# Attention's last ten units as five two-head units with side-by-side products, and the chain's preparation moved behind the first half of a step

## The chip, the cores and the metric

One core of a Trainium2 chip. The metric is device time of one execution in microseconds (us), the median of several runs. A core has TensorE (PE, matrix products out of SBUF into PSUM), VectorE (DVE), ScalarE (ACT), GpSimd (POOL) and SyncE (SP, which issues most DMA transfers). Each engine works through its own instructions in order and waits for semaphores of the others.

## The reference, cut to what matters

A two-layer backbone on 2048 latent and 256 context tokens. Each layer projects its input, runs a state-space scan (SSD), a gated delta rule (GDN) and attention beside each other, and multiplies the mix with `w_out`. Attention has 6 query heads of 64 over 2 key heads; GDN runs over chunks of 64 in both directions.

```python
def _attend(q, k, v):          # per block of 128 queries
    s = jnp.einsum('bqhgd,bkhd->bhgqk', qi, k) * scale
    pr = jax.nn.softmax(s, axis=-1)
    return jnp.einsum('bhgqk,bkhd->bqhgd', pr, v)

def step(S, inp):              # GDN, one chunk of 64
    v_new = u_i - jnp.einsum('bhcd,bhde->bhce', w_i, S)
    o = jnp.einsum('bhcd,bhde->bhce', qd, S) + jnp.einsum('bhij,bhje->bhie', a_i, v_new)
    S = S * d_i[..., None, None] + jnp.einsum('bhcd,bhce->bhde', kd, v_new)
```

## The kernel before, in words

Everything is fp32. A product on TensorE is either fp32, which the trace shows as two records per product, or fp32r, one record. Where more precision than one fp32r product gives is wanted, an operand is split into a rounded part and a remainder, and three fp32r products take the place of one fp32 product.

**Order of the work.** The program is emitted by Python loops. A planner then simulates it with its own costs and fixes each engine's order ahead of the run: of the instructions that are ready in its simulation it takes the one emitted first, those under `tc.high_priority()` ahead. `behind(a, b)` (L1002) adds an order between two instructions of one engine without a semaphore. Pools give each tile name a number of buffers (`bufs`); a tile waits for the release of the buffer before it.

**Attention** (L645) has 24 units per layer, one for each head and block of 512 queries, over 18 key tiles of 128. (Layer 0 has six small ones for the context tokens too.) For each unit `unit_max` (L515) loads the queries (`q2`, three buffers), lets GpSimd copy 64 rows of them to `qm` (L522), computes rough scores (`pq`, L531), takes their maxima on VectorE (`mx`, L533; `nm`, L535, L536), and turns the negative maxima into a row by four fp32 products with a one-column operand (`pm`, L541), which VectorE copies into row 64 of `qm` (L542). `unit_main` (L545) then goes over the key tiles: two score products (L562, L563), the exponential on ScalarE (`pe`, L565), and the product with the values (`po`, L556). The values have a 65th column of ones, which gives the row sums. For units 0 to 12 the value product is one fp32 product of a 65-column operand; for units 13 to 23 ScalarE rounds `pe` to `ph` (L570), VectorE makes the remainder `pl` (L571), and three fp32r products follow. The next unit's `unit_max` is advanced between a unit's key tiles. The scores and rough scores share three PSUM banks in the chain's stage.

**Around it.** Units 0 to 7 are emitted behind gating, `gdn_pre`, `gdn_solve`, `ssd_states` (its state product L789 writes two 64-column halves) and `ssd_out`; then comes `gdn_chain` (L1006), and the rest of the units behind it. So attention fills what these leave.

**The chain** goes over 18 tiles, both directions at once. In round u it emits the loads of tile u+2 (`load`, L1038, three buffers for `kqc`, `er`, `acv`), then `prep` of tile u+1 (L1058), then `step` of tile u (L1088). `prep` multiplies keys and queries by decays (L1060 on VectorE, L1062 and L1064 on GpSimd), masks `acv` (L1065 on VectorE), and completes an inverse by 32 small products (L1071, L1080) with ScalarE copies (L1075, L1083). `step` has two halves: products with the state (L1104), a subtraction (L1108), products (L1113, L1118), a copy (L1123), products (L1127, L1129), and the state's update on VectorE (L1131); GpSimd scales the old state (L1106).

The output product (L1238) of all tiles follows when the chain and attention allow.

Of the kernel before, what the change touches and what calls it, by code (L numbers as in the profile page):

```python
# [17 lines left out]
P = 128  # L18
# [16 lines left out]
GT = 768  # L35

# [48 lines left out]
def hybrid_kernel(ctx, tc, x, c, ctx_in, c_ctx, norm_w, w_mod, b_mod, w_in, conv_w, conv_b, ssd_A_log,  # L85
# [158 lines left out]
    for l in range(DEPTH):  # L244
# [246 lines left out]
        with ExitStack() as bx:  # L491
            splx = bx.enter_context(ExitStack())
            ap_ = splx.enter_context(tc.tile_pool(reuse_waits="tile", name="ap", bufs=2))
            spl = splx.enter_context(tc.tile_pool(reuse_waits="tile", name="spl", bufs=2))
            vh = []
# [19 lines left out]

            def unit_max(h, q0, qn, k0t, k1t, st):
# [4 lines left out]
                qm = ap_.tile([65, 512], F32R, name="qm", bufs=3)  # L521
                nc.gpsimd.tensor_copy(qm[0:64, :qn], q2[0:64, :qn].bitcast(F32))  # L522
# [3 lines left out]
                nm = ap_.tile([P, 4], F32, name="nm")  # L526
                for u in range(qn // P):
                    mx = ap_.tile([P, 8], F32, name="mx", bufs=4)
                    for i, (a, n) in enumerate(pieces):
# [3 lines left out]
                        nc.vector.tensor_reduce(mx[:, i:i + 1], pq[:, :n], axis=AX.X, op=ALU.max)  # L533
# [6 lines left out]
                for u in range(qn // P):  # L540
# [4 lines left out]
            def unit_main(h, q0, qn, k0t, k1t, st, sp=()):  # L545
# [5 lines left out]
                def pv():  # L551
                    kt, pe, ph, pl = pend.pop(0)
                    vs = slice(kvh * 64, kvh * 64 + 65)
                    ops = [(v1, pe)] if ph is None else [(vh[0], ph), (vh[1], ph), (vh[0], pl)]
                    for j, (v, p) in enumerate(ops):
                        nc.tensor.matmul(po[0:65, :qn], v[:, kt, vs], p[:, :qn], start=(kt == k0t and j == 0),  # L556
                                         stop=(kt == k1t - 1 and j == len(ops) - 1))

                for kt in range(k0t, k1t):
# [13 lines left out]
                    if len(pend) > (3 if sp else 1):  # L573
                        pv()
# [48 lines left out]
            def attention():  # L623
# [25 lines left out]
                for i, un in enumerate(big):  # L649
# [17 lines left out]
                    if i >= 14:  # L667
                        next(side_work, None)
# [642 lines left out]
```

## Time and profile before

| | us |
|---|---|
| median of 3 runs | 4003.42 (3998.72 to 4008.57) |
| profiled execution, its own time | 3989.31 |
| span of the profiled execution, first to last instruction | 3987.5 |
| mean granted share of TensorE's clock | 0.975 |

The profile is one execution. Busy times are of one engine's instructions; matrix products overlap in TensorE's pipeline and their ends are modelled, so the time from one start to the next is what a product costs in a full row. "Idle before" is the time in which an engine had nothing running ahead of an instruction, and the arrow names what released it.

### The profile page before, as it was taken

The numbers are of one execution on the slowest core, as the hardware profiler recorded it, in microseconds if no ns is written. First come the engines' busy times: TensorE is split into PE (matmuls) and PEld (weight loads), VectorE is DVE, ScalarE is ACT, GpSimd is POOL, SyncE is SP. The second block draws the span as 40 slices with busy tenths as digits, with TensorE's granted clock in tenths as the row PEclk, the third lists the DMA queues.
The fourth block names the chain that finished last, engine by engine and source line by source line (L and its number), as shares of the span: only waits on it lengthen the run. The fifth ranks groups of instructions, "written<-read, shape, count | busy, mean of one in ns | idle before, by whom it ended". The sixth has DMA issues, their size and how long they took to land. (4 is left out here: it accounts for less than half of the span.)

```text
span 3987.5 us, 70354 instructions
## 1 busy us (share of the span) xinstructions
PE 3758.9 (94%) x25750; PEld 2817.7 (71%) x25750; DVE 2704.5 (68%) x5372; ACT 1799.1 (45%) x3728; POOL 1347.3 (34%) x1762
## 2 busy tenths in 40 slices
PE   7999999988999898898999999999989999999989
PEld 5899999554466565565678999996544666656667
DVE  7556474789878566784547574755889876777733
ACT  5343342433466465574214443423333665566710
POOL 5112030376477322412213040302874662133010
PEclk8999999999999999998999999999999999999999
DMA  6343432354222654535744433332442226454244
GB/s 204 99 142 117 135 101 98 96 152 150 72 61 59 121 130 111 134 90 159 240 149 131 149 113 125 119 109 68 148 147 86 59 59 140 110 129 101 82 143 154
DMA packets 549798, 477.72 MB, mean 120 GB/s; under 512 B 133128, under 2 KB 487372, under 8 KB 549452
## 3 DMA queue, kind: packets, MB, share of 16 engines
q1 hardware_dynamic: 507596, 437.82, 37.6%
q10 hardware_dynamic: 41856, 35.40, 2.9%
q8 instruction: 203, 3.33, 0.3%
q14 instruction: 143, 1.17, 0.1%
HBM read 328.91 MB, written 144.18 MB: 119 GB/s over the span
## 5 line engine op out<-in xcount | busy, mean ns | idle before, releaser
L565 ACT ACTIVATE pe<-pst 128x512 f32<-128x512 f32 (+1 forms) x876 | 512.2, 594 | 619.7 <-PE pst L563 588.7
L533 DVE TENSOR_REDUCE mx<-pq 128x1 f32<-128x512 f32 (+1 forms) x972 | 589.5, 626 | 115.7 <-PE pq L531 112.0
L531 PE MATMUL pq<-khh,q 128*128 128x512 f32 (+1 forms) x972 | 456.6, 498 | 43.6 <-DVE mx L533 38.2
L556 PE MATMUL po<-pe,v 128*65 128x512 f32 x960 | 489.0, 598 | 1.8 <-ACT os__11676 L579 1.2
L562 PE MATMUL pst<-q,khh 128*128 128x512 f32 (+1 forms) x876 | 429.0, 490 | 25.5 <-DVE mx L533 23.2
L455 PE MATMUL ps<-lo,wh 128*128 128x384 f32 (+2 forms) x1296 | 441.2, 340 | 0.0
L455 PE MATMUL ps<-hi,wl 128*128 128x384 f32 (+2 forms) x1296 | 441.0, 340 | 0.0
L455 PE MATMUL ps<-hi,wh 128*128 128x384 f32 (+2 forms) x1296 | 440.9, 340 | 0.0
L401 PE MATMUL ps<-wh,hi 128*128 128x320 f32 (+1 forms) x1120 | 354.2, 318 | 1.3 <-DVE hi L365 1.2
L563 PE MATMUL pst<-qm,klo 65*128 65x512 f32 (+1 forms) x876 | 353.8, 405 | 0.0
L401 PE MATMUL ps<-wh,lo 128*128 128x320 f32 (+1 forms) x1120 | 350.0, 315 | 0.7 <-DVE lo L366 0.7
L401 PE MATMUL ps<-wl,hi 128*128 128x320 f32 (+1 forms) x1120 | 350.6, 314 | 0.0
L571 DVE TENSOR_TENSOR pl<-pe,ph 128x512 fp32r<-128x512 f32 x396 | 296.7, 755 | 72.3 <-ACT ph L570 38.2
L531 PEld LDWEIGHTS pq<-khh,q 128*128 128x128 f32 x972 | 184.8, 192 | 205.5 <-DVE mx L533 84.3
L376 DVE TENSOR_TENSOR wl<-wt,wh 128x1024 fp32r<-128x1024 f32 (+3 forms) x144 | 176.4, 1254 | 159.4 <-ACT wh L375 159.4
L570 ACT CAST ph<-pe 128x512 fp32r<-128x512 f32 x396 | 242.9, 620 | 61.0 <-DVE pl L571 21.9
L562 PEld LDWEIGHTS pst<-q,khh 128*128 128x128 f32 x876 | 168.4, 192 | 135.3 <-issue 53.9
L556 PE MATMUL po<-ph,vh 128*65 128x512 f32 x792 | 256.4, 405 | 1.3 <-ACT ph L570 0.7
L455 PEld LDWEIGHTS ps<-lo,wh 128*128 128x128 f32 x1296 | 244.0, 188 | 10.7 <-issue 0.4
L455 PEld LDWEIGHTS ps<-hi,wl 128*128 128x128 f32 x1296 | 243.4, 188 | 10.4
L455 PEld LDWEIGHTS ps<-hi,wh 128*128 128x128 f32 x1296 | 243.5, 188 | 10.3
L1238 PE MATMUL psd<-woh,mh 128*128 128x512 f32 x544 | 220.9, 406 | 18.1 <-ACT mh L1229 16.6
(588 smaller groups left out, 8094.2 us busy)
## 6 DMA issues: line engine op xcount, KB each, us to landing
wt<-in_w_in_dram SPq DMA_DIRECT2D x72, 512.0 KB
wmt<-in_w_mod_dram SPq DMA_DIRECT2D x48, 512.0 KB
pre_d<-pre SPq DMA_DIRECT2D x34, 512.0 KB
acv<-pre_d SPq DMA_DIRECT2D x34, 512.0 KB
kqc<-kt_d SPq DMA_DIRECT2D x68, 256.0 KB
acv<-pre_d SPq DMA_DIRECT2D x68, 256.0 KB
wt<-in_w_in_dram SPq DMA_DIRECT2D x24, 668.0 KB
wt<-in_w_in_dram SPq DMA_DIRECT2D x24, 640.0 KB
```

Of the source, the lines that this page charges most:

```text
L376: nc.vector.tensor_tensor(out=wl[:, ks, :], in0=wt, in1=wh[:, ks, :].bitcast(F32), op=ALU.subtract)
L401: nc.tensor.matmul(ps, hh[:, k, a], ww[:, k, :], start=(n == 0), stop=(n == 3 * KD - 1))
L455: nc.tensor.matmul(ps, ww[:, k, m * P:(m + 1) * P], hh[:, k, s0:s0 + sn], start=(n == 0), stop=(n == 3 * KD - 1))
L531: nc.tensor.matmul(pq[:, :n], q2[:, u * P:(u + 1) * P], khh[:, kvh, k0t * P + a:k0t * P + a + n], start=True, stop=True)
L533: nc.vector.tensor_reduce(mx[:, i:i + 1], pq[:, :n], axis=AX.X, op=ALU.max)
L556: nc.tensor.matmul(po[0:65, :qn], v[:, kt, vs], p[:, :qn], start=(kt == k0t and j == 0), stop=(kt == k1t - 1 and j == len(ops) - 1))
L562: nc.tensor.matmul(pt[:, :qn], khh[:, kvh, ks], q2[:, :qn], start=True, stop=False)
L563: nc.tensor.matmul(pt[:, :qn], klo[:, kvh, ks], qm[:, :qn], start=False, stop=True)
L565: nc.scalar.activation(out=pe[:, :qn], in_=pt[:, :qn], func=AF.Exp, scale=0.125)
L570: nc.scalar.copy(out=ph, in_=pe)
L571: nc.vector.tensor_tensor(out=pl, in0=pe, in1=ph.bitcast(F32), op=ALU.subtract)
L1238: nc.tensor.matmul(ps, a, w[k][:, n * 512:n * 512 + 512], start=(k == 0 and i == 0), stop=(k == KD - 1 and i == 2))
```

## The change

Five things, all in attention and the chain:

1. Units 0 to 13 stay as they are (unit 13 now with one fp32 value product); units 14 to 23 become five pairs of heads. A pair makes the scores of both heads for a key tile, and both exponentials into one tile `pe` of 128x2x512 (six buffers). The value products are fp32 with 64 columns of values; head 0 writes partitions 0 to 63 of `po`, head 1 partitions 64 to 127. They come in visits of two key tiles, with high priority, ordered behind the latest score product. Row sums no longer come from a column of ones: VectorE adds up the exponentials in `acc`, and two products with ones give the sums at the end.
2. The splitting for value products (`vh`, `ph`, `pl`) is gone.
3. The negative maximum of a unit is one reduction with `negate` into column 64 of a zeroed 65-column tile; four fp32r products turn it, and ScalarE copies the row into `qm`. The first 64 rows of `qm` come by a transfer of their own instead of GpSimd's copy.
4. `q2` and `qm` have four buffers instead of three.
5. In the chain, round u emits the loads of tile u+2, the first half of `step` of tile u, `prep` of tile u+1, and the second half. In `prep`, the two VectorE operations are ordered behind the state update of that first half, and the first set of small products behind its last product.

```diff
 def unit_max(h, q0, qn, k0t, k1t, st):
-    q2 = ap_.tile([P, 512], F32R, name="q2", bufs=3)
+    q2 = ap_.tile([P, 512], F32R, name="q2", bufs=4)
+    qm = ap_.tile([65, 512], F32R, name="qm", bufs=4)
     with tc.high_priority():
         nc.sync.dma_start(q2[:, :qn].bitcast(F32), qt_d[:, h, q0:q0 + qn])
-    nc.gpsimd.tensor_copy(qm[0:64, :qn], q2[0:64, :qn].bitcast(F32))
+        nc.sync.dma_start(qm[0:64, :qn].bitcast(F32), qt_d[0:64, h, q0:q0 + qn])
...
-        nc.vector.tensor_reduce(nm[:, u:u + 1], mx[:, 0:len(pieces)], axis=AX.X, op=ALU.max)
-    nc.vector.tensor_scalar(out=nm[:, :qn // P], in0=nm[:, :qn // P], scalar1=-1.0, scalar2=None, op0=ALU.mult)
+    nz = nmz[next(turn) % 2]
+    nc.vector.tensor_reduce(nz[:, 0:nu, 64:65], mx[:, 0:nu, 0:len(pieces)], axis=AX.X, op=ALU.max, negate=True)
...
-        nc.tensor.matmul(pm[64:65, u * P:(u + 1) * P], nm[:, u:u + 1], ident, start=True, stop=True)
-    nc.vector.tensor_copy(qm[64:65, :qn], pm[64:65, :qn])
+        nc.tensor.matmul(pm[0:65, u * P:(u + 1) * P], nz[:, u, :], identr, start=True, stop=True)
+    nc.scalar.copy(out=qm[64:65, :qn], in_=pm[64:65, :qn])

 def unit_main(...):
-        ops = [(v1, pe)] if ph is None else [(vh[0], ph), (vh[1], ph), (vh[0], pl)]
...
-            nc.scalar.copy(out=ph, in_=pe)
-            nc.vector.tensor_tensor(out=pl, in0=pe, in1=ph.bitcast(F32), op=ALU.subtract)
...
+def pair_main(h0, q0, qn, k0t, k1t, st):
...
+    def visit(n, behind_mm):
+        with tc.high_priority():
+            for v in range(n):
+                kt, pe = pend.pop(0)
+                for j in range(2):
+                    c0 = kvh[j] * 65
+                    mm = nc.tensor.matmul(po[half[j]], v1[:, kt, c0:c0 + 64], pe[:, j], start=(kt == k0t), stop=(kt == k1t - 1))
+                    if v == 0 and j == 0:
+                        behind(mm, behind_mm)
+    for kt in range(k0t, k1t):
+        pe = ap_.tile([P, 2, 512], F32, name="pe", bufs=PB)
+        for j in range(2):
+            pt = aslot("pst")
+            nc.tensor.matmul(pt, khh[:, kvh[j], ks], st["q2"][j], start=True, stop=False)
+            mm = nc.tensor.matmul(pt, klo[:, kvh[j], ks], st["qm"][j], start=False, stop=True)
+            nc.scalar.activation(out=pe[:, j], in_=pt, func=AF.Exp, scale=0.125)
...
+        elif kt == k0t + 1:
+            acc = ap_.tile([P, 2, 512], F32, name="acc", bufs=1)
+            nc.vector.tensor_tensor(out=acc, in0=pend[0][1], in1=pe, op=ALU.add)
+        else:
+            nc.vector.tensor_tensor(out=acc, in0=acc, in1=pe, op=ALU.add)
+        pend.append((kt, pe))
+        if len(pend) == 3:
+            visit(2, mm)
+        yield
+    visit(len(pend), mm)
+    nc.scalar.copy(out=os_, in_=po)
+    for j in range(2):
+        nc.tensor.matmul(pl[half[j]], cc("ones")[:, 0:64], acc[:, j], start=True, stop=True)
...
 def attention():
+    units = [(1, un) for un in big[:NS]] + [(2, un) for un in big[NS::2]]
...
-    def prep(u, xu, xt, kq, er, acv):
+    def prep(u, xu, xt, kq, er, acv, after=None):
-        nc.vector.tensor_tensor(out=kq[:, 0], in0=kq[:, 0], in1=er, op=ALU.mult)
+        ins = nc.vector.tensor_tensor(out=kq[:, 0], in0=kq[:, 0], in1=er, op=ALU.mult)
+        if after:
+            behind(ins, after[0])
...
+                    if after:
+                        behind(mm, after[1])
...
-        cur, nxt = nxt, prep(*ahead.pop(0)) if ahead else None
-        S, ox = step(u, S, *cur)
+        st = step(u, S, *nxt)
+        after = next(st)
+        if ahead:
+            nxt = prep(*ahead.pop(0), after)
+        S, ox = next(st)
```

## Rows read from the trace of the kernel before

**Rows 1.** The page: busy time, share of the span and instructions of each engine.

```profile
PE 3758.9 (94%) x25750; PEld 2817.7 (71%) x25750; DVE 2704.5 (68%) x5372; ACT 1799.1 (45%) x3728; POOL 1347.3 (34%) x1762
```

**Rows 2.** Windows by stage: window, length, busy us (instructions) per engine, clock, DMA.

```profile
core 0: us, PE busy (x) PEld busy (x) DVE busy (x) ACT busy (x) POOL busy (x), PEclk, DMA share, GB/s
700.00:1100.00 400.00, 367.76 (x1774) 208.06 (x1773) 342.38 (x771) 160.06 (x356) 233.06 (x350) 0.96 0.38 117
1340.00:1730.00 390.00, 347.70 (x4973) 230.58 (x4975) 270.87 (x507) 232.26 (x454) 116.34 (x103) 0.96 0.55 124
1730.00:1830.00 100.00, 96.26 (x437) 63.61 (x438) 75.67 (x127) 75.24 (x128) 4.55 (x4) 0.98 0.25 76
```

**Rows 3.** Timeline of TensorE, a split unit: start, us, line, operation, shapes, count.

```profile
1782.94 0.62 PE L556 MATMUL po<-ph,vh 128*65 128x512 f32 x2
1783.40 0.40 PE L556 MATMUL po<-pl,vh 128*65 128x512 f32 x1
```

**Rows 4.** Timeline of TensorE in an unsplit unit: four fp32 records and what follows.

```profile
951.43 1.88 PE L556 MATMUL po<-pe,v 128*65 128x512 f32 x4
953.24 0.55 PE L789 MATMUL pst<-xd,bn 128*64 128x192 f32 x4
```

**Rows 5.** Timeline of VectorE in the chain stage, layer 0.

```profile
1475.04 0.41 DVE L1131 TENSOR_TENSOR Sc<-sd,p 128x256 f32<-128x256 f32 x1
...
1483.17 0.41 DVE L1131 TENSOR_TENSOR Sc<-sd,p 128x256 f32<-128x256 f32 x1
1487.33 0.69 DVE L1060 TENSOR_TENSOR kqc<-kqc,er 128x512 f32<-128x512 f32 x1 [3.74 <-DMA kqc<-kt_d]
...
1495.35 0.41 DVE L1131 TENSOR_TENSOR Sc<-sd,p 128x256 f32<-128x256 f32 x1
...
1679.13 0.69 DVE L1060 TENSOR_TENSOR kqc<-kqc,er 128x512 f32<-128x512 f32 x1 [2.52 <-DMA kqc<-kt_d]
...
1688.98 0.42 DVE L1131 TENSOR_TENSOR Sc<-sd,p 128x256 f32<-128x256 f32 x1
...
1712.18 0.42 DVE L1131 TENSOR_TENSOR Sc<-sd,p 128x256 f32<-128x256 f32 x1
1720.81 0.41 DVE L1131 TENSOR_TENSOR Sc<-sd,p 128x256 f32<-128x256 f32 x1
...
1730.63 0.42 DVE L1131 TENSOR_TENSOR Sc<-sd,p 128x256 f32<-128x256 f32 x1 [0.32 <-PE p L1129]
```

**Rows 6.** Timeline of SyncE, which issues the loads.

```profile
1482.48 0.58 SPq L1054 DMA_DIRECT2D kqc<-kt_d  x1
```

**Rows 7.** L1060, idle before it by releaser (us, times): both layers.

```profile
  DMA kqc<-kt_d: 44.4, 15
  DMA kqc<-kt_d: 32.5, 14
```

**Rows 8.** Timeline of TensorE: eight records of L789 and what follows.

```profile
946.50 0.87 PE L789 MATMUL pst<-xd,bn 128*64 128x192 f32 x8
947.30 0.66 PE L776 MATMUL pt<-cst,xb 128*128 128x128 f32 x4
```

**Rows 9.** L789 weight loads, 900 to 1000 us: duration ns min/median/max, first, last start.

```profile
L789 PEld LDWEIGHTS pst<-xd,bn x88: 132/136/231, 939.0 to 998.8; 128*64 128x64 f32 x88
```

**Rows 10.** Timeline of TensorE: transposition of a unit's maxima.

```profile
1483.78 1.03 PE L541 MATMUL pm<-cst,nm 128*1 128x128 f32 x8
1484.74 0.50 PE L562 MATMUL pst<-q,khh 128*128 128x512 f32 x1
```

**Rows 11.** Timeline of TensorE in projection: five fp32r transpositions and what follows.

```profile
292.74 0.54 PE L326 MATMUL ptq<-identr,hl 128*128 128x128 f32 x5
293.12 0.38 PE L401 MATMUL ps<-wh,lo 128*128 128x320 f32 x1
```

**Rows 12.** VectorE by line, 1340 to 1730 us: busy us, mean ns | idle.

```profile
L571 DVE TENSOR_TENSOR pl<-pe,ph 128x512 fp32r<-128x512 f32 x143 | 110.7, 780 | 14.6 <-ACT ph L570 6.4 <-PE po L556 4.8 <-ACT pe L565 1.0
```

**Rows 13.** The page's costliest groups: an element-wise operation of 128x1024 on VectorE.

```profile
L376 DVE TENSOR_TENSOR wl<-wt,wh 128x1024 fp32r<-128x1024 f32 (+3 forms) x144 | 176.4, 1254 | 159.4 <-ACT wh L375 159.4
```

More of the change, by code (lines that the diff above doesn't have):

```diff
@@ L35 @@
 GT = 768
+PB = 6
+NS = 14
 def rev(t):
@@ L582, in unit_main, with pair_max @@
                 nc.sync.dma_start(mx_d[640 + h * 64:704 + h * 64, q0:q0 + qn], os_[ob:ob + 64, :qn])
+                yield
+            def pair_max(h0, q0, qn, k0t, k1t, st):
+                st.update(q2=[], qm=[])
+                gens = []
+                for j in range(2):
+                    sj = {}
+                    g = unit_max(h0 + j, q0, qn, k0t, k1t, sj)
+                    for i, _ in enumerate(g):
+                        if i == 0:
+                            st["q2"].append(sj["q2"])
+                            st["qm"].append(sj["qm"])
+                        yield
@@ L625, in attention @@
                 small = [] if last else [(h, 0, LC, 0, TC) for h in range(HQ)]
-                sb, ss_ = [{} for _ in big], [{} for _ in small]
-                mb = [unit_max(*un, st) for un, st in zip(big, sb)]
+                units = [(1, un) for un in big[:NS]] + [(2, un) for un in big[NS::2]]
+                sb, ss_ = [{} for _ in units], [{} for _ in small]
+                mb = [(unit_max if n == 1 else pair_max)(*un, st) for (n, un), st in zip(units, sb)]
                 ms = [unit_max(*un, st) for un, st in zip(small, ss_)]
@@ L648, in attention @@
                         pass
-                for i, un in enumerate(big):
-                    if i == 13:
-                        for _ in range(2):
-                            vh.append(spl.tile([P, NT, 129], F32R, name=f"vh{len(vh)}", bufs=1))
-                        nc.scalar.copy(out=vh[0], in_=v1)
-                        nc.vector.tensor_tensor(out=vh[1], in0=v1, in1=vh[0].bitcast(F32), op=ALU.subtract)
-                    spn = () if i < 13 else range(NT)
+                at = 0
+                for i, (n, un) in enumerate(units):
                     nxt = ms[i:i + 1] + mb[i + 1:i + 2]
-                    left = (21 + 3) * (i + 1 < len(big)) + 3 * (i < len(small))
+                    left = (24 * units[i + 1][0] if i + 1 < len(units) else 0) + 6 * (i < len(small))
+                    steps = n * (NT - 4)
                     done = 0
-                    for j, _ in enumerate(unit_main(*un, sb[i], spn)):
-                        want = left * (j + 1) // (NT - 4)
+                    for j, _ in enumerate((unit_main if n == 1 else pair_main)(*un, sb[i])):
+                        want = left * (j + 1) // steps
                         adv(nxt, want - done)
@@ L666, in attention @@
                             pass
-                    if i >= 14:
-                        next(side_work, None)
-                    if i % HQ == HQ - 1:
-                        if small and i == HQ - 1:
+                    at += n
+                    for k in range(at - n, at):
+                        if k >= 14:
+                            next(side_work, None)
+                    if at % HQ == 0:
+                        if small and at == HQ:
                             inv(0, LC)
-                        inv(big[i][1], 512)
+                        inv(un[1], 512)
                     yield
```

72 lines of the change are left out of this document (44 added, 28 removed).

## The prediction

> **What bounds the kernel now.** I read the busy shares first: TensorE is busy for 94% of the span, VectorE for 68% [rows 1]. TensorE's ends are modelled, so 94% is not proof. Then the windows by stage [rows 2], which split one layer's attention. From 700 to 1100 us VectorE (342 of 400) is nearly as full as TensorE. In the chain's stage, 1340 to 1730, TensorE is busy for 348 of 390 and VectorE for 271. In the rest of attention, 1730 to 1830, TensorE has 96 of 100. So TensorE leads from the chain's start to attention's end, and what it is spared or stops waiting for there is time. Projection and the output product are not touched by the diff.
>
> Next I read TensorE's timeline for the pace of a product, from start to start. Two 512-column products of a split unit start 0.46 us before the next, 0.23 each [rows 3]. The unsplit fp32 product is two records; four records (two key tiles) hold TensorE for 1.81 us, so one key tile costs 0.87 with some change-over in it [rows 4].
>
> Last I read the chain on VectorE [rows 5]. The state update (L1131) comes twice per tile. From a first to a second half it takes 8.1 us (1475.04 to 1483.17), from that second half to the next first (1495.35) 12.2 us; ten steps, from 1475.04 to 1688.98, take 21.4 us each. In the 12.2 us VectorE stands still for 3.74 us in front of L1060, the decay multiply of `prep`, until a load of `kqc` lands. That load was issued at 1482.48 [rows 6], 4.85 us before. Whose multiply is it? The last of the 18 runs at 1679.13, while the last tile's two updates come at 1720.81 and 1730.63: each multiply is planned two tiles ahead, right after the load that has only just got its buffer (three of them). It is needed a whole step later, but VectorE works in order, so all that is queued behind it waits, the chain's own subtraction (L1108) among it. This is 44.4 us in 15 waits in layer 0 and 32.5 in 14 in layer 1 [rows 7]. Near the end, with no load left, a second-to-first interval is 8.6 us (1712.18 to 1720.81).
>
> **The change part by part, per layer.**
>
> *PV products.* Ten units of 18 key tiles at three products go: 10 x 18 x 3 x 0.23 = 124 us. In their place five pairs, whose two heads use the two column halves of the array. The nearest row is the state product of `ssd_states` (L789): 128 rows by 64 columns, fp32, two neighbours in different halves. Eight records of 192 columns take 0.80 us from start to the next product's start [rows 8]. One after another they would take 8 x 192/512 x 0.43 = 1.29; two by two 0.65. So they run side by side, and 0.15 is left for going into and out of the half-array form. For 512 columns I take 0.87 us per key tile for both heads: 5 x 18 x 0.87 = 78, and one more pair of products for the row sums, 5 x 0.87 = 4. Saved: 42. The diff gathers two key tiles in a visit, so a pair has nine visits and the sums, ten change-overs; I take 0.3 each, twice the row, because the products in front and behind lose a little too: +15. Bounds 0.15 to 0.5: +7 to +25.
>
> *Unit 13* becomes unsplit: 18 x (0.87 - 0.69) = +3.
>
> *The maximum's transposition.* Eight fp32 records hold TensorE for 0.96 us (1483.78 to 1484.74) [rows 10]; the nearest row for four fp32r products of 128 columns is L326, five in 0.38 [rows 11], so 0.3. I add 0.2 for the one-column form that goes, an estimate from the 0.15 of [rows 8]. Saved 0.85 us per unit: 9 us in the last ten units. For the 14 earlier ones 12 us, of which I count 6, since VectorE shares the bound there. VectorE itself loses five small operations and the copy of the maxima, which goes to ScalarE (half idle, [rows 1]); GpSimd's copy of `qm` becomes a 128 KB transfer. I cost these at nothing. What hides the transfer is the query load already queued in front of it; without that cover it is one more load like the one of [rows 6], under 5 us at a unit's start.
>
> *Splitting.* 11 x 18 = 198 casts leave ScalarE and as many subtractions of 0.78 us (L571 [rows 12]) leave VectorE. In come 17 additions of 128x1024 per pair. The nearest row is L376, 1.25 us [rows 13]: 5 x 17 x 1.25 = 106 against 154. VectorE gets lighter by 48 us, the waits of products for `pl` fall away, since PV now needs only the exponential. Against: an addition is longer than a subtraction, and a chain operation behind it waits up to 1.25 instead of 0.78. With 4 chain operations in each of 18 steps and half of the 0.47 each, that is 17 us if the chain were the bound; TensorE has other work meanwhile. Taken: +5, bounds 0 and +17.
>
> *Preparation behind half a step.* L1060 and L1065 are held behind the state update of the first half, the first products of `prep` behind that half's last product. By then the load has had more than a step. The stall of VectorE goes: 3.0 us per tile by [rows 7]. Upper bound: the step falls from 21.4 to twice 8.6, 4.2 us x 16 = 67 us. Lower bound: nothing, if the two multiplies (0.69 each), 32 small products and their ScalarE copies simply lengthen the first half; VectorE would then come late to L1108 by some 1.4 us, and TensorE would wait as it waits now. I take 40 us, close to the two rows' mean of 38: the stall is idle time of an engine in order, and the preparation itself is not new work. GpSimd's share of `prep` (L1062, L1064) is not held and may still wait for the load; its only chain operation, L1106, is wanted half a step later at the state update, so I cost that at nothing; without that room it is the same 3 us on another engine. On SP the loads are emitted where they were. A wait moved is L1060's: queued behind it on VectorE are maxima and additions, and the next half's subtraction.
>
> *Query buffers.* A pair holds two of four, the next pair's maxima the other two; so the load for the pair after can only start when a pair ends, where one of three buffers was spare before. At each of four changes of pair TensorE may wait for a load: 0 to 4.85 us [rows 6]. Taken 2: +8.
>
> Sum per layer: -42 + 15 + 3 - 9 - 6 + 5 - 40 + 8 = -66, for two layers -132. The profiled execution took 3989.3 us, so 3857; the median of the runs lies 14 above the profiled one, so **3871 us** as a median.
>
> **Rivals.**
>
> *The preparation's gain is lost.* It is as long between the halves as between the steps, and TensorE waits there. Then the 40 us fall away: -26 per layer, 3951. For: the multiplies are emitted ahead of the second half, so VectorE takes them first. Against: the update needs TensorE for the second half's products anyway, during which VectorE would have little of the chain to do.
>
> *Everything lands.* The step falls to 17 us, the maxima's 12 us count in full, buffers and additions cost nothing: -42 + 15 + 3 - 21 - 67 = -112 per layer, 3779. For: TensorE's pool of attention work can fill any hole. Against: VectorE then has its whole remaining work in a shorter stage (271 - 30 of some 310), and holes appear on both engines.
>
> *The halves don't run side by side at 512 columns.* In the row both neighbours read moving tiles of 192 columns; here each streams 512 from two places of one large tile. If TensorE takes them in turn, a key tile costs 1.74 for the pair, 82 us more per layer: **4035 us, slower** by 0.8%. It decides as soon as the two heads' records start more than about 0.35 us apart instead of some ns. Against: [rows 8], where 0.80 us hold what would take 1.29.
>
> *The weight loads show.* Each record brings its own 64 columns of weights. If they are not hidden beside products of the other half, four loads of 0.136 us [rows 9] per key tile and pair come on top: 4 x 0.136 x 18 x 5 = 49 per layer, 3969. For L789 eight loads alone would be 1.09 us one behind the other, and loads and products together take 0.80 [rows 8, 9]. The Trainium skill, page TensorE: Matmul & The Clock Gate, Part 3 (Packing small matmuls), says that weight loads overlap with matmuls in flight only where the row group differs; here both heads use all the rows. By that rule this rival would be the likely one; the row speaks against it.
>
> *The change doesn't do it.* The planner puts the held multiplies so late, or the load comes so late behind SP's other work, that the wait only moves, and pairs lose in holes what they gain: 4000.
>
> **How the numbers follow.** Forecast (3820 to 3920) 0.47; preparation's gain lost 0.20; everything lands 0.17; serial halves 0.07; loads show 0.03; no effect 0.06. What a measurement can tell from no change is about 0.3%, 12 us. Faster: 0.47 + 0.20 + 0.17 + 0.03 = 0.87; same 0.06; slower 0.07. Leaving out the serial rival, the no-effect one and the lower part of "everything lands" (some 0.2 together) gives 3790 to 3965.
>
> **What would show it.** In the changed kernel's trace: L1060 without idle time before it, and both kinds of interval between state updates at 8 to 10 us; the two heads' products starting some ns apart and nine visits of about 1.7 us plus change-over per pair; the maxima's products at 0.3 us; TensorE's stage from the chain's start to attention's end shorter by 55 to 70 us in each layer. The prediction is wrong if the first-half interval grows by what the other loses, if VectorE's busy share in the chain's stage passes 85% with TensorE falling, or if products wait for query loads at changes of pair by more than 3 us.

## The result and the profile after

The changed kernel takes **3913.3 us** (median of 4 runs, 3905.2 to 3913.5) against 4003.3: a ratio of 0.9774, 95% interval 0.9758 to 0.979. Forecast were 3871, range 3790 to 3965. So 90 us came of 132. In the experiments below one execution of e7 took 9502 us and is left out, and no trace of e7 is read. The profiled execution took 3913.4 us with a span of 3911.5; its line of busy shares, to be held against [rows 1]:

```profile
PE 3685.5 (94%) x25190; PEld 2710.5 (69%) x25190; DVE 2580.1 (66%) x4886; ACT 1599.1 (41%) x3384; POOL 1325.0 (34%) x1712
```

TensorE's busy time fell by 73 us and the span by 76. So TensorE's idle time, 228.6 us before (3987.5 - 3758.9), is still 226.0. The prediction had counted on 40 us per layer of it. That is the question of this study: **the stall went away, and the idle time, over the whole span, didn't.**

By stage it moved. From the chain's start to attention's end, windows of layer 0 and layer 1 in the kernel before, then in the changed one:

```profile
1366.00:1828.60 462.60, 422.59 (x5147) 280.47 (x5147) 332.72 (x612) 295.18 (x557) 113.62 (x102) 0.97 0.45 109
3332.00:3803.80 471.80, 435.27 (x5106) 291.72 (x5104) 333.71 (x611) 295.81 (x557) 110.67 (x99) 0.97 0.44 108
1396.00:1779.60 383.60, 349.96 (x4834) 203.14 (x4832) 269.59 (x411) 178.10 (x357) 110.30 (x96) 0.94 0.57 132
3344.00:3705.00 361.00, 342.88 (x4742) 200.25 (x4740) 266.51 (x404) 175.38 (x351) 102.56 (x91) 0.97 0.57 135
```

Window less TensorE's busy time, that is 40 and 37 us of idle time before (the prediction's 40 per layer would have been all of it), 34 and 18 after: 25 us less. In the stages ahead of the two chains it rose from 106 to 126 us, behind attention from 46 to 48.

First, what came as forecast. VectorE's timeline in the chain (start, us, line, operation, shapes, count; L1193 is the state update, old L1131; L1116 and L1123 are the old L1060 and L1065), and the totals of the multiply L1116 over both layers:

```profile
1501.35 0.42 DVE L1193 TENSOR_TENSOR Sc<-sd,p 128x256 f32<-128x256 f32 x1 [0.70 <-PE p L1191]
1501.69 0.68 DVE L1116 TENSOR_TENSOR kqc<-kqc,er 128x512 f32<-128x512 f32 x1
1502.29 0.69 DVE L1123 TENSOR_TENSOR acv<-acv,msk 128x512 f32<-128x512 f32 x1
...
1516.82 0.41 DVE L1193 TENSOR_TENSOR Sc<-sd,p 128x256 f32<-128x256 f32 x1
...
1524.62 0.41 DVE L1193 TENSOR_TENSOR Sc<-sd,p 128x256 f32<-128x256 f32 x1
...
1532.77 0.41 DVE L1193 TENSOR_TENSOR Sc<-sd,p 128x256 f32<-128x256 f32 x1
```

```profile
L1116 DVE TENSOR_TENSOR kqc<-kqc,er x36: 679/686/1424, 1387.3 to 3639.5; 128x512 f32<-128x512 f32 x36
...
  DMA kqc<-kt_d: 2.9, 2
```

The multiply stands right behind the first half's update and waits for nothing; 76.9 us of waits in [rows 7] are 2.9. The halves take 7.8 and 8.2 us (1516.82 to 1524.62 to 1532.77), a tile 15.5 (1501.35 to 1516.82) where [rows 5] had 21.4. Over the whole chain of layer 0 the gain is smaller: 20.0 us per tile instead of 20.8. Now a visit of a pair and the maxima's products, in TensorE's timeline:

```profile
1479.32 1.08 PE L634 MATMUL pl<-acc,cst 128*64 128x512 f32 x4
1480.33 0.50 PE L613 MATMUL pst<-q,khh 128*128 128x512 f32 x1
...
1509.77 0.45 PE L546 MATMUL pm<-identr,nmz 128*65 128x128 f32 x4
1510.06 0.45 PE L613 MATMUL pst<-q,khh 128*128 128x512 f32 x1
...
1513.71 0.40 PE L614 MATMUL pst<-qm,klo 65*128 65x512 f32 x1
1513.94 0.52 PE L536 MATMUL pq<-khh,q 128*128 128x512 f32 x2
...
1515.98 0.40 PE L614 MATMUL pst<-qm,klo 65*128 65x512 f32 x1
1516.31 1.94 PE L604 MATMUL po<-pe,v 128*64 128x512 f32 x8
1518.18 0.50 PE L536 MATMUL pq<-khh,q 128*128 128x512 f32 x1
```

A visit is eight records: two key tiles, two heads, two records each. They hold TensorE for 1.87 us (1516.31 to 1518.18). Eight, one after another, would take some 3.4 to 3.6 (8 x the prediction's 0.43; [rows 4] has 1.81 for four), so **the halves run side by side at 512 columns too**, and the weight loads are hidden. By the rule of the Trainium skill that the prediction weighed (page TensorE: Matmul & The Clock Gate, Part 3), these loads would have shown; this row speaks against it, as [rows 8] did. The two products with ones at a pair's end (L634) are four records of the same form and hold TensorE for 1.01 us (1479.32 to 1480.33). So four records more cost 0.86, and 1.87 less twice 0.86 leaves 0.15 us lost behind the visit. A product like the one in front gives way to the next after 0.23 us (1513.71 to 1513.94); here it takes 0.33, so 0.10 are lost ahead. 0.25 in all, 0.3 forecast. The maxima's four products take 0.29 us, 0.3 forecast.

Then, where it did not come. The stage of the chain by windows (0.93 is the granted clock; [rows 2] had 0.96):

```profile
1396.00:1747.00 351.00, 320.11 (x4716) 190.06 (x4716) 244.63 (x385) 155.16 (x320) 107.04 (x94) 0.93 0.58 130
1440.00:1460.00 20.00, 14.93 (x167) 8.68 (x169) 11.65 (x19) 5.04 (x10) 6.55 (x6) 0.67 0.33 79
```

A hole of TensorE reaches into the last row's window. The same moment on three engines, from three timelines (in square brackets the idle time before, and what ended it):

```profile
1441.61 1.26 POOL L1122 TENSOR_TENSOR kqc<-kqc,er 128x512 f32<-128x512 f32 x1 [13.96 <-DMA xt__13473<-xd_d]
1442.83 1.66 POOL L111 TENSOR_TENSOR sso<-sso,mhalf 128x8 f32<-128x8 f32 x1
```

```profile
1444.52 0.17 DVE L1220 TENSOR_TENSOR sso<-sso,rqr 128x8 f32<-128x8 f32 x1 [12.62 <-POOL sso L111]
1444.60 0.42 DVE L1193 TENSOR_TENSOR Sc<-sd,p 128x256 f32<-128x256 f32 x1
1444.93 1.42 DVE L1116 TENSOR_TENSOR kqc<-kqc,er 128x512 f32<-128x512 f32 x1
```

```profile
1445.07 1.12 PE L1166 MATMUL p<-Sc,kqc 64*64 64x64 f32 x16 [12.77 <-DVE Sc L1193]
```

Read from the top: GpSimd's multiply L1122 (old L1064) stands ahead of its turn and waits 14 us for a load (the profile names that of `xt_`, which `load` emits together with the multiply's own operands). Behind it is the reciprocal root of the output's norm (L111), for which VectorE's L1220 waits; behind that is the state update, and for this TensorE waits 12.8 us. In the window from 1440 to 1460, whose first 5 us are the end of the hole, the clock is 0.67. L1220's waits of this kind, over both layers (us, times):

```profile
  POOL sso L111: 31.9, 7
```

Last, the stages, from the first or last record of each (us; layer 0 / layer 1):

| | before | after |
|---|---|---|
| first maxima product of attention | 559 / 2571 | 704 / 2683 |
| first state copy (`ssd_states`) | 935 / 2947 | 1004 / 2983 |
| chain, first state update | 1366 / 3332 | 1396 / 3344 |
| chain, last state update | 1731 / 3693 | 1747 / 3672 |
| attention's last unit | 1829 / 3804 | 1780 / 3705 |
| last output product | 2091 / 3982 | 2056 / 3906 |

From the chain's start to attention's end the time fell by 79 and 111 us; "55 to 70" was the mark. But, counted from each layer's start, attention begins 145 and 147 us later, the states 69 and 71, the chain 30 and 47. From each layer's start to attention's end only 49 and 64 us are left (66 were forecast), and behind it 14 and 23 us are lost again. Nothing in the prediction speaks of these late starts.

### The profile page after: what moved, and what is told of

Read it like the earlier page. It is cut to its first block, busy times and chain, and to the rows that moved or that the text cites. A ratio compares the mean times of both kernels' runs of the same rounds, so it can differ in the third digit from the quotient of the medians.

```text
span 3911.5 us, 68050 instructions
## 1 busy us (share of the span) xinstructions
PE 3685.5 (94%) x25190; PEld 2710.5 (69%) x25190; DVE 2580.1 (66%) x4886; ACT 1599.1 (41%) x3384; POOL 1325.0 (34%) x1712
## 5 line engine op out<-in xcount | busy, mean ns | idle before, releaser
L558 PE MATMUL po<-pe,v 128*65 128x512 f32 (+1 forms) x1032 | 525.6, 597 | 1.6 <-ACT os__12287 L574 0.9
L536 PE MATMUL pq<-khh,q 128*128 128x512 f32 (+1 forms) x972 | 464.6, 519 | 51.7 <-DVE mx L538 42.1
L566 ACT ACTIVATE pe<-pst 128x512 f32<-128x512 f32 (+1 forms) x516 | 300.3, 591 | 463.4 <-PE pst L564 460.1
L563 PE MATMUL pst<-q,khh 128*128 128x512 f32 (+1 forms) x516 | 284.7, 553 | 30.2 <-DVE mx L538 28.0
L615 ACT ACTIVATE pe<-pst 128x512 f32<-128x512 f32 x360 | 206.3, 597 | 174.3 <-PE pst L614 171.3
L624 DVE TENSOR_TENSOR acc<-acc,pe 128x1024 f32<-128x1024 f32 x160 | 208.6, 1303 | 59.7 <-ACT pe L615 57.8
L1305 PE MATMUL psd<-woh,ml 128*128 128x512 f32 x544 | 217.3, 400 | 0.6
L1305 PE MATMUL psd<-wol,mh 128*128 128x512 f32 x544 | 217.1, 399 | 0.0
L377 ACT CAST wh<-wt 128x1024 fp32r<-128x1024 f32 (+3 forms) x144 | 145.9, 1056 | 172.6 <-PE ps L457 151.3
```

The source lines that it names most:

```text
L377: nc.scalar.copy(out=wh[:, ks, :], in_=wt)
L536: nc.tensor.matmul(pq[:, :n], q2[:, u * P:(u + 1) * P], khh[:, kvh, k0t * P + a:k0t * P + a + n], start=True, stop=True)
L558: nc.tensor.matmul(po[0:65, :qn], v1[:, kt, kvh * 64:kvh * 64 + 65], pe[:, :qn], start=(kt == k0t), stop=(kt == k1t - 1))
L563: nc.tensor.matmul(pt[:, :qn], khh[:, kvh, ks], q2[:, :qn], start=True, stop=False)
L566: nc.scalar.activation(out=pe[:, :qn], in_=pt[:, :qn], func=AF.Exp, scale=0.125)
L615: nc.scalar.activation(out=pe[:, j], in_=pt, func=AF.Exp, scale=0.125)
```

## The experiments

All times are medians; each ratio is to the kernel before, run beside it on the same chip. Not all runs were on one chip, so the ratios are the safer measure of a difference between two versions; where they say something else than the medians, both are given. "Corrections" are changes to the changed kernel.

| | us | ratio (95%) |
|---|---|---|
| changed kernel | 3913.3 | 0.9774 (0.9758 to 0.979) |
| e1 GpSimd held | 3881.2 | 0.9697 (0.9669 to 0.9726) |
| e2 pairs only | 4018.1 | 1.0036 (1.0023 to 1.0049) |
| e3 moved preparation only | 3908.5 | 0.9763 (0.9735 to 0.979) |
| e4 four buffers | 3883.2 | 0.9706 (0.9682 to 0.973) |
| e5 both corrections | 3867.0 | 0.9663 (0.9649 to 0.9677) |
| e6 preparation, held, no pairs | 3903.6 | 0.9757 (0.9743 to 0.9772) |
| e7 e5, visits of one key tile | 3886.1 | 0.9709 (0.9692 to 0.9725) |
| e8 pairs only, four buffers | 4004.8 | 1.0006 (0.9997 to 1.0016) |
| e9 e6 and the new maxima | 3861.4 | 0.9652 (0.9631 to 0.9672) |
| e10 e5, reciprocal deferred | 3853.4 | 0.963 (0.9612 to 0.9648) |
| e11 e10 with 7 pairs | 3882.2 | 0.9703 (0.9684 to 0.9722) |
| e12 e10, pairs in a pool of their own | 3812.4 | 0.9536 (0.9518 to 0.9555) |

Theory A at the start: the rest of the gain is lost at GpSimd's share of `prep`, which the prediction had cost at nothing. Rival B: the attention's larger pool delays the stages ahead of the chain. Rival C: the pairs cost more than forecast.

**e1, GpSimd held.**

```diff
-nc.gpsimd.tensor_tensor(out=kdw, ...)
+ins = nc.gpsimd.tensor_tensor(out=kdw, ...)
+if after:
+    behind(ins, after[2])
...
```

The same for `kq[:, 1]`; `after[2]` is `sd` of the first half, which `step` now hands out too.

> The changed kernel with GpSimd's two multiplies of the next tile's preparation (L1120, L1122) also held, behind the first half's own GpSimd operation (the decayed state sd). Theory A: the part of the gain that did not arrive is GpSimd's unheld share: it waits for the kqc load, GpSimd works in order, and VectorE's L1220 then waits for the reciprocal root behind it (31.9 us in 7 waits in the two layers), TensorE with it, and the granted clock falls to 0.67 in the 20 us that follow the longest wait. Then the waits at L1220 go below 5 us, the clock of layer 0's chain stage rises from 0.94 to 0.97, and the time is 3875 to 3895 (25 us of idle and clock, at the middle 3885). Rival B: these waits are hidden by other work of TensorE, and the lost part lies before and behind the chain: 3908 to 3918, no difference.

3881: 32 us less (31 by the ratios, 18 to 44 with both intervals). L1220 stands in line 1224 here, and the windows of the chain's stage and of the same 20 us follow:

```profile
  POOL sso L111: 3.0, 5
```

```profile
1396.00:1728.00 332.00, 319.08 (x4711) 189.38 (x4704) 247.56 (x385) 154.28 (x319) 111.99 (x94) 0.95 0.61 137
1440.00:1460.00 20.00, 19.90 (x280) 11.58 (x277) 13.26 (x19) 9.14 (x19) 3.87 (x4) 0.93 0.78 175
```

The waits are gone (31.9 to 3.0), TensorE has 19.9 of these 20 us instead of 14.9, and the stage takes 332 us instead of 351. Theory A holds: **the term cost at nothing was 32 us**. Of the clock's recovery only half came (0.95, not 0.97).

**e2, pairs only.** The chain as before, the rest of the change as it is.

```diff
-st = step(u, S, *nxt)
-after = next(st)
-if ahead:
-    nxt = prep(*ahead.pop(0), after)
+cur, nxt = nxt, prep(*ahead.pop(0)) if ahead else None
+st = step(u, S, *cur)
+next(st)
```

> The changed kernel with the chain's preparation as before (whole step ahead, nothing held); pairs, maxima and buffers stay. By the prediction's terms without the 40 us per layer: 3989 - 52 + 14 = 3951. Theory A (GpSimd's unheld share eats most of what the moved preparation gives, the pairs give what was forecast): 3940 to 3955. Rival C (the additions, change-overs and query buffers cost more than forecast and the moved preparation gives its 40 us per layer): 3985 to 3995.

4018, outside all ranges: alone the pairs, with the new maxima and buffers that stay in, make the kernel **slower**, by 0.2 to 0.5%. The chain's stage (1404 to 1797), and the two largest waits of VectorE there that a load ends:

```profile
1404.00:1797.00 393.00, 340.75 (x4600) 198.74 (x4601) 239.57 (x376) 146.24 (x300) 105.48 (x91) 0.84 0.50 110
```

```profile
DVE acv L1123 <- DMA acv<-pre_d: 43.5, 13, 4.7
...
DVE kqc L1116 <- DMA kqc<-kt_d: 11.9, 11, 3.2
```

VectorE stands still in front of the loads as it did before. TensorE has less to fill the hole with: it is idle for 52 of 393 us instead of 36 of 365 (1366 to 1731), and its clock is 0.84 instead of 0.97. Where a stall of another engine sets the pace, the time that TensorE is spared turns into idle time and a lower clock.

**e3, the moved preparation only.** The kernel before with `prep`, `step` and the loop of the changed one.

> The kernel before with only the chain's preparation moved behind half a step. By the prediction's term of 40 us per layer: 4003 - 80 = 3923. Theory A: GpSimd's multiply is pulled ahead here too and TensorE's idle time in the chain's stage (42 us per layer, of which the pairs had a share) bounds the gain: 3960 to 3980. Rival C: 3920 to 3935.

3908: the move alone gives as much as the whole change, and more than rival C's 3920 to 3935; theory A's 3960 to 3980 is refuted. By the ratio it is 95 us (84 to 106). Between the profiled executions it is 80 (3987.5 to 3907.6), the 2 x 40 of the prediction; but the profiled execution of the kernel before is 14 us faster than its median. So A holds for the changed kernel (e1) and not for the move by itself, and C is right that the pairs don't pay in the changed kernel.

```profile
1362.00:1699.00 337.00, 329.65 (x4838) 225.79 (x4837) 275.37 (x508) 229.98 (x450) 109.81 (x101) 0.98 0.57 133
1699.00:1790.00 91.00, 85.98 (x354) 56.19 (x353) 65.27 (x108) 66.14 (x114) 3.59 (x3) 0.96 0.25 79
```

TensorE is idle for 12 us of these two stages; before it was 40. It has split units to work on, and hardly waits for anyone.

**e4, four buffers of the exponentials.**

```diff
-PB = 6
+PB = 4
```

> The changed kernel with four instead of six buffers of the exponentials (PB = 4), 8 KB less per partition. Theory A: room in SBUF is not what is short: 3910 to 3920, a little slower where a pair waits for a buffer. Rival B: the tiles of the state and output stages (first state copies at 1004 us instead of 935) wait for the room that the attention's larger pool takes; then these copies come back to about 940 to 970 us, the chain starts 20 us earlier, and the time is 3880 to 3895.

3883: 30 us less (27 by the ratios), as rival B said. The state copies, in the changed kernel and with four buffers (duration min/median/max, first and last start):

```profile
L834 ACT COPY xn<-pt x18: 478/478/480, 1004.0 to 1082.0; 128x384 f32<-128x384 f32 x18
```

```profile
L834 ACT COPY xn<-pt x18: 472/479/481, 927.7 to 1021.6; 128x384 f32<-128x384 f32 x18
```

They start 76 us earlier, the chain 65 (1331 instead of 1396). So rival B holds beside e1's theory A. The diff shows the size of it: `pe` goes from 4 x 2 KB to 6 x 4 KB per partition, `acc`, `os2` and `sm_` add 8, `q2` and `qm` 4, the maxima's tiles 2, against 26 KB of `spl` that go: 4 KB more than before.

**e5, both corrections.** The edits of e1 and e4.

> The changed kernel with both corrections: GpSimd's share of the preparation held, and four buffers of the exponentials. If the two losses are separate (theory A and rival B were each about 30 us): 3845 to 3860. If both only make room for the same work of TensorE, or for the same rise of its granted clock: 3868 to 3885.

3867, between the two expectations and at the edge of the second: 46 us of 62. A wait that took time stands in the timelines of VectorE and TensorE:

```profile
1367.02 0.30 DVE L693 RECIPROCAL sm<-sm 128x24 f32<-128x24 f32 x1 [12.45 <-DMA sm<-sm_d]
```

```profile
1367.66 1.12 PE L1170 MATMUL p<-Sc,kqc 64*64 64x64 f32 x16 [10.62 <-DVE Sc L1197]
```

The reciprocal of the row sums waits for its own load. Over both layers VectorE stood still before it for 23.7 us in the changed kernel, 22.5 in e1, 28.0 in e4 and 37.2 here, and the longest of these waits now lies in the chain (12.45 us; 6.1 in the changed kernel). It is the same pattern for the third time: an engine in order, a load just issued, and the state update queued behind.

**e6, preparation and hold without pairs.** The kernel before with the edits of e3 and e1.

> The kernel before with the moved preparation and GpSimd's share held, no pairs. Theory: without the pairs TensorE has enough attention work per step to cover GpSimd's waits (the move alone left under 6 us of waits of TensorE in layer 0's chain stage), so holding gives little: 3898 to 3910, against 3908 for the move alone. Rival: the held multiplies are worth the same 30 us here: 3872 to 3885. Either way, the difference to the run with both corrections is what the pairs give when nothing else is in their way; forecast were 26 us per layer, 52 in all.

3903.6: holding gives 5 us here by the medians and 2 by the ratios, which can't be told from nothing. But the reason is not the expected one, that TensorE covers GpSimd's waits. Without pairs VectorE hardly waits for the reciprocal root, though nothing is held; in e3 (line L1164 there) over both layers:

```profile
  POOL sso L109: 0.7, 2
```

That is against 31.9 us in the changed kernel, and 2.1 with the pairs alone (e2): it takes the pairs and the moved preparation together. GpSimd's longest wait for a semaphore in front of its multiply is 4.4 us in e3 and 13.5 in the changed kernel. Why it is longer there was not tested.

**e7, visits of one key tile.**

```diff
-if len(pend) == 3:
-    visit(2, mm)
+if len(pend) == 2:
+    visit(1, mm)
```

> The kernel with both corrections, with visits of one key tile instead of two: 18 visits per pair and the sums instead of 9 and the sums, 9 change-overs more in each of 5 pairs and 2 layers, 90 in all. By the 0.3 us of the prediction 27 us slower than the run with both corrections; by the 0.25 us read in the changed kernel's timeline (0.10 ahead of the visit, 0.15 behind it) 22 us; if the change-overs lie in TensorE's idle time, under 8 us.

The ratios differ by 0.0046, 18 us for 90 change-overs: 0.20 us each, 0.1 to 0.3 with both intervals. The timeline's 0.25 lies within, and so does the prediction's 0.3. Rival C has no ground in the change-overs.

**e8, pairs only, four buffers.** The edits of e2 and e4.

> The pairs alone (preparation as before) with four buffers of the exponentials. If the larger pool of the attention costs its 30 us here too: 3985 to 3992, and the pairs alone are still worth only some 15 us of the 52 forecast, because the chain's stage is set by the waits on VectorE and a shorter TensorE only waits longer, at a lower clock (0.84 in layer 0's chain stage). If the late state stage is what made the pairs alone slower altogether: 3945 to 3960.

4004.8, above both expectations: the room gives 13 us here. Without the moved preparation the pairs and the new maxima together are worth nothing (1.0006, 0.9997 to 1.0016) even where the state stage has room.

**e9, the new maxima without pairs.** The kernel of e6 with the `unit_max` of the changed kernel (four buffers of `q2` and `qm` included).

> The kernel before with the moved preparation, GpSimd's share held, and the new unit_max (maxima of four query blocks in one tile, fp32r transposition, copy on ScalarE, second query load, four query buffers); no pairs. By the prediction's terms for the maxima and the query buffers, 2 x (-9 - 6 + 8) = -14 against the move with hold (3903.6): 3890. If the buffers cost nothing and the earlier units count in full: 2 x -21 = -42: 3862. If TensorE's time for the maxima lies beside VectorE's in the units before the chain: 3895 to 3905. What is left to the run with both corrections (3867) is the pairs' own.

3861, the second expectation: 42 us less than e6, 20 less than e1, which has the pairs, and no more than e5, which has them and the room. It is the sum that the expectation has for maxima that count in full and buffers that cost nothing, but the sum doesn't show these two apart: in e9 the state stage starts late as well (first copies at 1015 us, the chain at 1407; e6 has 935 and 1361), so that the 42 us are what is left after a loss of unknown size. Of the stage of the chain:

```profile
1407.00:1733.60 326.60, 323.73 (x4814) 224.99 (x4813) 260.02 (x460) 236.36 (x467) 107.78 (x92) 0.99 0.59 137
```

TensorE is busy for 99% of it at a clock of 0.99; e1, which differs by the pairs and their pool, has 319 of 332 at 0.95. So up to here the pairs, with the pool as it was, had **cost** 20 us (3861 to 3881; 18 by the ratios).

**e10, the reciprocal deferred.**

```diff
-nc.vector.reciprocal(sm[:, :w], sm[:, :w])
-nc.sync.dma_start(sr_d[fl]..., sm[:, :w])
+late.append((sm, fl, w))
...
+if j == 12 and n == 2:
+    put(adds[-1])
```

`put` emits reciprocal and store, behind an addition of the next pair.

> The kernel with both corrections, and the reciprocal of the row sums (L693) of a finished row of units emitted in the middle of the next pair, behind one of its additions, instead of right behind its own load. In the run with both corrections VectorE stood still before it for 12.45 us at 1367 us and 5.61 us at 1596 us, with holes of 10.6 and 5.3 us on TensorE, and 4.15 us in layer 1. If these holes are on the path: 3843 to 3857. If other attention work fills them later: 3861 to 3870, no difference.

3853: 14 us less, so the holes were on the path. The three waits that the expectation names, 22 us of VectorE's, are gone. With e1 and e4 that makes 60 us; that it is so near the 62 is partly chance, since part of the reciprocal's wait was in the changed kernel from the start.

**e11, seven pairs.** `NS = 10` in the kernel of e10.

> The same with 7 pairs instead of 5 in each layer (NS = 10), so that four units ahead of the chain become pairs. If a pair gives what the five gave (37 us for ten pairs in two layers, with the maxima in it): 13 us less than the run with the deferred reciprocal. If the pairs ahead of the chain give nothing, since VectorE bounds there (342 of 400 us busy) and an addition for two heads is 1.30 us: no difference, or up to 10 us slower.

29 us slower, worse than any expectation. From the gate to the chain's start, with 7 pairs and with 5:

```profile
725.00:1352.00 627.00, 580.37 (x2824) 343.37 (x2824) 518.09 (x1070) 301.62 (x744) 392.06 (x509) 0.95 0.36 106
```

```profile
725.00:1331.00 606.00, 569.18 (x2789) 339.98 (x2788) 480.72 (x1033) 302.56 (x745) 385.48 (x510) 0.98 0.37 109
```

VectorE gets 37 us more to do in a stage where it is nearly full, TensorE's idle time rises from 37 to 47 us, and its clock falls. A pair's place is where VectorE has room.

**e12, the pairs' tiles in a pool of their own**, opened behind the units' pool, as `spl` was.

```diff
+pp = splx.enter_context(tc.tile_pool(reuse_waits="tile", name="pp", bufs=2))
-pe = ap_.tile([P, 2, 512], F32, name="pe", bufs=PB)[:, 0]
+pe = ap_.tile([P, 512], F32, name="pe", bufs=3)
-pe = ap_.tile([P, 2, 512], F32, name="pe", bufs=PB)
+pe = pp.tile([P, 2, 512], F32, name="pe2", bufs=PB)
-sm_ = ap_.tile([65, 512], F32, name="sm_", bufs=1)
+sm_ = ap_.tile([65, 512], F32, name="os_", bufs=1)
```

`acc` and `os2` go into `pp` as well.

> The kernel with the deferred reciprocal (3853), with the pairs' own tiles in a pool of their own that is opened behind the pool of the units, as the tiles of the split products were before, and with 4 KB less of them (three buffers of a unit's exponentials, the row sums of a pair in the units' output tile). In the kernel before, and in the run with the new maxima and no pairs, the first unit's first maxima product starts at 559 us, in the changed kernel and in the run with both corrections at 704: with the pairs' tiles in the same pool it reaches over room that projection still uses. If that late start is what the pairs still cost: the first product starts near 560 us again, and the time is 3832 to 3846, of which 11 us would be the TensorE idle time that the two stages up to the gate have grown by (31.1 - 27.0 and 17.7 - 10.6). If the start only shifts work from one full stage to the other: 3849 to 3858.

**3812**: 41 us less than e10 (38 by the ratios), where 7 to 21 were expected. The maxima's products ahead of 760 us, in the changed kernel and here; then e12's busy line and its stage of the chain:

```profile
L536 PE MATMUL pq<-khh,q x42: 277/542/801, 704.3 to 754.9; 128*128 128x512 f32 x32, 128*128 128x256 f32 x10
```

```profile
L538 PE MATMUL pq<-khh,q x51: 275/397/802, 559.7 to 759.4; 128*128 128x512 f32 x38, 128*128 128x256 f32 x13
```

```profile
PE 3643.1 (96%) x25190; PEld 2683.4 (70%) x25190; DVE 2566.3 (67%) x4886; ACT 1596.3 (42%) x3384; POOL 1334.4 (35%) x1712
...
1336.00:1643.00 307.00, 298.57 (x4663) 180.71 (x4663) 237.04 (x387) 145.72 (x303) 107.88 (x93) 0.99 0.67 150
```

The first unit starts at 560 us again, TensorE's idle time is 166.7 us (e10: 186.4), and 307 us are left of the chain's stage. Counted from the edits, e12 takes 4 KB more per partition than e10 in all, so it is the place of the tiles and not their amount that brings the start back. The edit changes three things at once (the pool, the width and number of the units' buffers, the tile of the sums), and 41 us are the price of all three; the expectation counted TensorE's idle time ahead of the gate alone, and what the rest came from was not separated. This is the fastest version, 4.6% below the kernel before and 101 us below the changed one (95 by the ratios), with all the parts of the change in it.

## Why the prediction came near, and where it failed

The forecast was 42 us short of the measured time (3871 against 3913), and it is so near because larger errors of both signs meet. That it lies in the part of the range that was held most likely (3820 to 3920) is luck: the number is as near to the rival of a lost preparation (3951), and in fact the rest of the change added nothing to the preparation's gain (e3). Its terms, for both layers:

| step of the prediction | forecast | measured |
|---|---|---|
| preparation moved, VectorE's stall | -80 | -95 between medians, -80 between profiled executions (e3) |
| GpSimd's share of it, "I cost that at nothing" | 0 | +32 in the changed kernel (e1), none that can be told without pairs (e6) |
| maxima (-30) and query buffers (+16) | -14 | -42, with a late state stage in it (e6 to e9) |
| pairs, change-overs, unit 13, additions | -38 | +20 as the change has them (e9 to e1) |
| room for the larger pool | not in the sum | 14 to 30 for the state stage (e5, e4), 41 for e12's edit (e10 to e12) |

The steps from run to run add up to the whole change: -95 (e3), -5 (e6), -42 (e9), +20 (e1), +32 (without the hold) are -90. The last row is no further term; what it shows lies within the maxima's and the pairs' rows.

*Preparation.* Right in mechanism and near in size. But [rows 7] are not the whole stall. In the kernel before L1065 waits for loads too, 47.8 us over both layers, most of it for its own operand:

```profile
  DMA acv<-pre_d: 31.8, 17
```

The move took this as well (L1123 waits for no load of its tile in the changed kernel), so that 40 us read from one row came so near is in part luck. The rival that its gain is lost between the halves did not come: the halves take 7.8 and 8.2 us.

*GpSimd.* **This step failed.** The prediction named the unheld multiplies and gave even a price ("the same 3 us on another engine", per tile; 32 us over 36 tiles are 0.9), and then looked only at the state's decay (L1168) behind them. What it missed is that GpSimd also computes the norm's reciprocal root for `out`, and that VectorE waits for that with the state update queued behind. That this needs the pairs beside it (e6) stood nowhere either. A term is not nothing because one reader of the queue has room; every instruction queued there counts, and all who wait for them.

*Maxima and buffers.* Mis-sized. The 14 earlier units were counted by half because VectorE shares the bound, and 16 us were set aside for query loads. In e9 42 us came, as much as if all of it counted. The price per unit holds as far as it was read (0.29 us instead of 0.96); the 0.2 us for the one-column form were not measured. The wait for query loads, over both layers of the changed kernel (total, times, longest):

```profile
PE pq L536 <- DMA q<-qt_d: 4.8, 3, 1.8
```

That is 5 us where 16 were set aside.

*Pairs.* The price of the products was right to a few hundredths of a us: side by side, 0.86 us per key tile (the forecast's 0.87 is less than half of the 1.81 that [rows 4] give, without a working for it), change-over 0.20 to 0.25 instead of 0.3, additions of 1.30 us in the mean (1.23 at the median) for 1.25. It did not become time in the changed kernel: without the moved preparation the loads that VectorE waits for set the pace (e2, e8: nothing, or a loss), and with it they cost 20 us as long as their tiles lay in the units' pool (e9 to e1). Where these waits are gone and the tiles have room, e9 to e12 gives 49 us (46 by the ratios); but in e9 the state stage starts late too (1015 us), so part of the 49 is room, and the deferred reciprocal lies between the two as well. Room for that stage was worth 14 us (e1 to e5) to 30 (e4), which would leave 16 to 35 us for the pairs, of 38 forecast. A kernel with the new maxima, this room and no pairs was not run, so this stays an estimate.

*What stood in no step.* The diff takes a pool away and makes another larger, and the prediction read it for instructions alone. With 4 KB more the states start 69 us later in layer 0, with 4 KB less (e4) 7 us earlier. And since the pairs' buffers lie in the pool from which the first unit takes its query tile, that unit starts at 704 us instead of 559, though pairs come only ten units before the end. That the tiles wait for room which projection and `gdn_solve` still use is inferred: the runs show that a smaller pool brings the states' start back (e4) and separate pools attention's (e12).

*The rivals.* Serial halves, visible weight loads and a gain lost between the halves are refuted as mechanisms. "Everything lands" (3779 as a median) is nearest to what e12 shows, 3812, but e12 has four corrections that the change hasn't.

## What to carry to other kernels

Cost a moved step on every engine that it touches, by what is queued behind each of its instructions and who waits for that; a wait taken from one engine in order can come back on another, as it did here on GpSimd, or behind another load on the same one, as with the reciprocal. Read a diff for its pools as for its instructions: which stage starts in the room that it takes? And work that an engine is spared is time only in a stage where that engine ends last: unblock the slow dependency first, then shorten the products.

## What the runs showed of the hardware

- TensorE's granted clock falls in a hole, and stays low for a while beyond it. Behind the idle 12.77 us TensorE was busy throughout, first at 0.50, the lower of its two levels (1.2 GHz), and later at 1.00 (2.4 GHz):

```profile
1445.00:1451.00 6.00, 5.93 (x61) 3.63 (x63) 5.96 (x9) 1.32 (x3) 1.82 (x2) 0.50 0.24 69
1454.00:1460.00 6.00, 6.00 (x75) 4.01 (x76) 4.51 (x8) 3.65 (x7) 1.62 (x2) 1.00 0.57 127
```

  With the hole gone (e1), the window from 1440 to 1460 had 0.93 instead of 0.67. Over the chain's stage of layer 0 it was 0.97 before, 0.84 with the pairs alone, 0.99 in e9 and e12. So a hole costs more than its length.
- VectorE's operations on two SBUF operands of 128x512 can take longer when a GpSimd operation is already under way. L1116 takes 0.69 us at the median, and 1.42 at 1444.93, where GpSimd had begun an operation at 1444.76 and began the next at 1445.76. Where L1116 started first (1517.15, GpSimd's L1168 0.15 us later) it stayed at 0.68, and L1123, which started 0.60 us later into the same L1168, took 1.10. Not every operation does this: beside the small L111, L1116 and L1123 took 0.68 and 0.69 (1653.10, 1653.70). With GpSimd held behind the same update (e1), L1123, there L1127, took 1.10 us in 30 of its 34 runs (0.69 in the kernel before):

```profile
1444.76 1.04 POOL L1222 TENSOR_TENSOR zzg<-zzg,sso 128x512 f32<-128x512 f32 x1 [0.28 <-DVE sso L1220]
1445.76 1.06 POOL L1168 TENSOR_TENSOR sd<-Sc,dsc 128x256 f32<-128x256 f32 x1
...
L1127 DVE TENSOR_TENSOR acv<-acv,msk x34: 684/1102/1760, 1383.2 to 3618.3; 128x512 f32<-128x512 f32 x34
```

Preparation held behind the update on both engines now falls beside GpSimd's scaling of the state. What that costs in time was not measured by itself.
